# Encoder layer with neighbourhood attention and Fourier mixing: a third Y buffer, an earlier store, earlier squares and a moved scale

## The chip, the cores and the metric

The kernel runs on one core of a Trainium2 chip. The metric is the device time of one execution in microseconds (us); the time of a kernel is the median over its runs. All arithmetic is float32: a matrix product is done as three TensorE products of a high and a low part (high by high, high by low, low by high), so every operand is first split in two by ScalarE (a cast to the rounded type) and VectorE or GpSimd (the remainder). In the profile PE is TensorE, PEld its weight load, DVE is VectorE, ACT is ScalarE, POOL is GpSimd and SP is SyncE, whose queue issues nearly all DMAs.

## The reference

One encoder layer is applied to a prompt of 256 rows and a sample of 2048 rows, each row of width 1024.

```python
def encoder_layer(x, w_in, rpb, w_fourier, b_fourier, g_pre, g_na, g_f, w_out, g_post):
    h = rms_norm(x, g_pre)
    proj = h @ w_in
    q, k, v, z_a, u_f, z_f = jnp.split(
        proj, [NA_WIDTH, 2 * NA_WIDTH, 3 * NA_WIDTH, 4 * NA_WIDTH, 4 * NA_WIDTH + F_WIDTH], axis=-1)
    y_a = neighbourhood_attention(q, k, v, rpb)
    y_f = fourier_mix(u_f, w_fourier, b_fourier)
    mixed = jnp.concatenate([rms_norm(y_a, g_na) * jax.nn.silu(z_a),
                             rms_norm(y_f, g_f) * jax.nn.silu(z_f)], axis=-1)
    out = mixed @ w_out
    return x + rms_norm(out, g_post)
```

`neighbourhood_attention` works on a grid of 64 columns: each position attends to a window of up to 8 rows by 16 columns, with a bias from `rpb` and logits scaled by 1/8. `fourier_mix` takes the real part of a two-dimensional FFT over the sequence and over groups of 64 channels, then multiplies by `w_fourier` and adds `b_fourier`. All four widths (NA_WIDTH, F_WIDTH, and the heads and groups that make them up) come to 512.

## The kernel before, in words

The program is one straight line of instructions. Its stages, with the time at which they run in the profiled execution:

1. **Projections (0 to 555).** The columns of `w_in` are multiplied with the normalised rows. For the prompt this is a loop of 16 steps (the `for b in range(16)` loop at line 749): step `b` makes one block of 128 output columns, and `b // 4` tells which tensor it belongs to (two gates, then k, then q). The weights of step `b` are split two steps ahead by `b_raw(b)` (lines 574 to 584) into `wh` (ScalarE) and `wl` (VectorE; GpSimd for the steps listed in `WP`). For b of 12 and more, the q columns, the split also multiplies by -0.125. The result leaves PSUM through a ScalarE activation (line 783).
2. **Fourier stage two (555 to 580)**, which leaves its spectra in SBUF.
3. **The Y stage (580 to 616).** A loop over four blocks `e` of 128 channels (line 1315). For each block three products `ti` in the order 2, 0, 1 are made by `y_mm` into PSUM (`py`), biased by ScalarE into `t1`, and combined by VectorE into the tile `Y` of 128 x 2304 float32, 1152 KB in all (`comb`, line 1276). The first 256 columns, the prompt's, are stored to DRAM (`yD`) inside `y_out` as soon as `ti` 2 is done (line 1302), the other 2048 after the three (line 1325). `Y` has two buffers, so block 2 overwrites the tile of block 0 and block 3 that of block 1. For the first two blocks and part of the third, the squares of Y are summed into `sqs` (ScalarE squares, GpSimd adds). During block 2 a small tile `y0` is loaded: rows 0 to 127 of the first three Y blocks from `yD` (line 1321) and their gates from `zD` (line 1322). GpSimd multiplies the two (line 1324). During block 3 VectorE adds the fourth block (line 1348), ScalarE and VectorE split `y0` into `y0h` (lines 1350 and 1352), and the scores of the first two attention groups are worked in between. From here on the order on every engine is the order in which the code is written (`manual_schedule`); ahead of it the scheduler of the framework orders ACT, DVE, POOL and SP, while the order on TensorE is always as written.
4. **Attention with the output product of the Fourier half woven in (616 to 850).** `G` is a list of 36 groups (4 pairs of heads by 9: the prompt and 8 pieces of the sample). Step `k` (line 1575) does the transposes of group `k - 2` (`transp`: TensorE into `ptb`, then copies by ScalarE and VectorE into `pt`), the scores and exponentials of group `k`, and the product with v (`pv`). On even steps one output tile of 128 rows (`ftiles`) is multiplied by half of `w_out`: `f_mm` into two PSUM tiles, `f_evac` into `ofs`, stored to `oD`. The inputs of a tile are loaded by `ys_load` (`yr` from `yD`, `yz` from `zD`), multiplied by GpSimd (`ys_mul`) and split (`y_hi` on ScalarE, `y_lo` on VectorE). `pv` leaves a closure in `pending`, which `run_squares` calls in the next step: it squares the `pv` result on ScalarE. The PSUM slot of `pv` (tag "c") is a single one, so the next `pv` waits for that square.
5. **The attention half of the output product and the residual (850 to 947).**

The weights that stage 4 reads first, `wo1`, are loaded in two halves of 2 MB (`load_wo1(0)`, `load_wo1(1)`, line 1227), together with the bias table `tb` of the first pair of heads (`load_t(0, 1)`) and the q tiles of groups 2 and 3 (`prep`). All of them are issued on SP ahead of the Y stage.

Of the kernel before, what the change touches and what calls it, by code (L numbers as in the profile page):

```python
# [10 lines left out]
F32 = mybir.dt.float32  # L11
F32R = mybir.dt.float32r
AF = mybir.ActivationFunctionType
ALU = mybir.AluOpType
# [3 lines left out]
TP, TS = 256, 2048  # L18
T = TP + TS
# [6 lines left out]
NG = 13  # L26
NK = 16
BP = (3, 5)
WP = (7, 9, 11)

HALF = ((0, 28), (4, 8), (12, 16), (20, 24))
KW = (24, 32, 32, 24)
# [143 lines left out]
def build(tc, A, O):  # L176
    nc = tc.nc
# [396 lines left out]
    def b_raw(b):  # L574
        wh, wl = [gt(BS, F32R, "w" + x) for x in "hl"]
        src = wp_[b]
        if b < 12:
            nc.scalar.copy(wh, src)
            (nc.gpsimd if b in WP else nc.vector).tensor_tensor(out=wl, in0=src, in1=wh.bitcast(F32), op=ALU.subtract)
        else:  # L580
            nc.scalar.activation(wh, src, AF.Copy, scale=-0.125)
            nc.vector.scalar_tensor_tensor(out=wl, in0=src, scalar=-0.125, in1=wh.bitcast(F32), op0=ALU.mult,
                                           op1=ALU.subtract)
        wb[b] = wh, wl


# [162 lines left out]
    for b in range(16):  # L749
        kind, blk = divmod(b, 4)  # L750
        if b < 10:
            wz_load(1)
        if b in (0, 2):
            n_load((b // 2, 1))
        if b == 10:
            op_load(0)
        if b == 12:
            op_load(1)
        if b < 14:
            b_raw(b + 2)  # L760
        if b < 8:
            x, y = divmod(b, 2)
            n_scale(None, *divmod(x, 2)[::-1], range(2 * y, 2 * y + 2))
        elif b < 12:
            n_sum(b - 8)
        if b in (3, 5, 12, 13):
            n_first((3, 5, 12, 13).index(b))
        if b > 13:
            op_split(b - 14)
        p = mmt(512)[:, :TP]  # L770
        wh, wl = wb.pop(b)
        for k in range(KC):
            mm3(nc, p, wh[:, k], wl[:, k], hp_[:, k], lp_[:, k], k == 0, k == KC - 1)
        o = st.tile([128, 256], F32, tag="f", name="f", bufs=3)
        if kind == 1:
            v = [(o, p)]
        elif kind == 3:
            v = [(o[:, 128 * x:128 * x + 128].rearrange("p (x r c) -> p r x c", x=2, c=16),
                  p[:, 128 * x:128 * x + 128].rearrange("p (r x c) -> p r x c", x=2, c=16)) for x in range(2)]
        else:  # L780
            v = [(o.rearrange("p (r b c) -> p b r c", b=2, c=32), p.rearrange("p (b r c) -> p b r c", b=2, c=32))]
        for d, i in v:
            nc.scalar.activation(d, i, AF.Silu if kind < 2 else AF.Copy)
        if kind < 2:
            nc.sync.dma_start(zD[kind, blk * 128:blk * 128 + 128, :TP], o)
        else:
            nc.sync.dma_start((kD if kind == 2 else qD)[blk, :, :TP], o)
# [297 lines left out]
    def load_t(pr, kind):  # L1085
        t = TB[pr, kind] = tp.tile([128, 2400], F32, tag="tb", name="tb", bufs=2)
        if kind == 0:
            nc.sync.dma_start(t[:, :512], A["tp"][pr])
            nc.sync.dma_start(t[:, 512:1792].rearrange("p (h x) -> p h x", h=2), tD[pr][:, :, :640])
        else:  # L1090
            nc.sync.dma_start(t[:, :1760].rearrange("p (h x) -> p h x", h=2), tD[pr][:, :, 640:])
# [18 lines left out]
    def prep(g):  # L1110
        pr = g["pr"]
        ql = g["q"] = jl.tile([128, 256], F32, tag="q", name="q", bufs=4)
        if g["R"] is None:
            nc.sync.dma_start(ql, qD[pr, :, :TP])
            return
        for x, n, r in halves(g):
            t0 = TP + 1024 * (r // 16) + 512 * g["hc"]
            q = qD[pr, :, t0:t0 + 512].rearrange("p (b x) -> p b x", b=2)[:, :, 16 * (r % 16):16 * (r % 16) + n // 2]
            nc.sync.dma_start(ql.rearrange("p (b x) -> p b x", b=2)[:, :, x // 2:x // 2 + n // 2], q)
# [107 lines left out]
    def load_wo1(n):  # L1227
        for c in range(4):
            wo1[n].append(gt([128, 2, 512], F32R, "wo1"))
            nc.sync.dma_start(wo1[n][c].bitcast(F32),  # L1230
                              woD[1, :, c, :, n * 512:n * 512 + 512].rearrange("x p d -> p x d"))

    load_wo1(0)
    for g in G[:2]:
        prep_v(g)
    load_wo1(1)
    load_t(0, 1)
    prep(G[2])
    prep(G[3])
    pg = ExitStack()  # L1240
    sm = pg.enter_context(tc.tile_pool(name="smY", bufs=2))
    sqy = pq_.enter_context(tc.tile_pool(name="sqy", bufs=1, side="right"))
# [70 lines left out]

    order = ExitStack()
    for e in range(4):
        Y = sqy.tile([128, T], F32, tag="Y", name="Y", bufs=2)
        if e < 3:
            for ti in (2, 0, 1):
                y_out(e, ti, *y_mm(e, ti))
                if e == 2 and ti == 2:  # L1320
                    nc.sync.dma_start(y0[:, 0, :3], yD[1, :3, :, :128].rearrange("c p t -> p c t"))
                    nc.sync.dma_start(y0[:, 1], zD[0, :, :128].rearrange("(c p) t -> p c t", p=128))
                if e == 2 and ti == 0:
                    nc.gpsimd.tensor_tensor(out=y0[:, 0, :3], in0=y0[:, 0, :3], in1=y0[:, 1, :3], op=ALU.mult)
            nc.sync.dma_start(yD[1, e, :, TP:], Y[:, TP:])
            if e == 2:
                Y2 = Y
            for i in range(T // SQ if e < 2 else 1):
                ts = slice(i * SQ, i * SQ + SQ)
                if e == 0:  # L1330
                    nc.scalar.activation(sqs[:, ts], Y[:, ts], AF.Square)
                elif e == 2:
                    sq = sm.tile([128, SQ], F32, tag="sqf", name="sqf", bufs=2)
                    nc.scalar.activation(sq[:, :TP], Y[:, :TP], AF.Square)
                    nc.gpsimd.tensor_tensor(out=sqs[:, :TP], in0=sqs[:, :TP], in1=sq[:, :TP], op=ALU.add)
                else:
                    sq = sm.tile([128, SQ], F32, tag="sqf", name="sqf", bufs=2)
                    nc.scalar.activation(sq, Y[:, ts], AF.Square)
                    nc.gpsimd.tensor_tensor(out=sqs[:, ts], in0=sqs[:, ts], in1=sq, op=ALU.add)
            continue  # L1340
        order.enter_context(tc.manual_schedule(engines=MAN))
        py = y_mm(e, 2)
        scores(G[0])
        first_soft(G[0], lambda: y_out(e, 2, *py))
        py = y_mm(e, 0)
        y0h = gt([128, 2, 4, 128], F32R, "y0h")
        y0h = [y0h[:, 0], y0h[:, 1]]
        nc.vector.tensor_tensor(out=y0[:, 0, 3], in0=Y[:, :128], in1=y0[:, 1, 3], op=ALU.mult)
        sq = sm.tile([128, SQ], F32, tag="sqf", name="sqf", bufs=2)
        y_out(e, 0, *py, lambda: (nc.scalar.copy(y0h[0], y0[:, 0]),  # L1350
                                  nc.scalar.activation(sq[:, :TP], Y[:, :TP], AF.Square)))
        nc.vector.tensor_tensor(out=y0h[1], in0=y0[:, 0], in1=y0h[0].bitcast(F32), op=ALU.subtract)
        soft(G[0], 0)
        soft(G[0], 1)

        nc.sync.dma_start(y0[:, 0], yD[1, :, :, 128:256].rearrange("c p t -> p c t"))
        nc.sync.dma_start(y0[:, 1], zD[0, :, 128:256].rearrange("(c p) t -> p c t", p=128))
        scores(G[1])
        py = y_mm(e, 1)
        first_soft(G[1])  # L1360
        nc.vector.tensor_tensor(out=sqs[:, :TP], in0=sqs[:, :TP], in1=sq[:, :TP], op=ALU.add)
        soft(G[1], 0)
        y_out(e, 1, *py)
# [60 lines left out]
    def ys_split(d):  # L1424
        y_hi(d)
        y_lo(d)
# [25 lines left out]
    def f_evac(d, n):  # L1452
        t, p = d["t"], d.pop(("p", n))
        if n == 0:
            d["o"] = gt([128, D], F32, "ofs")
        o = d["o"]
        ns = slice(n * 512, n * 512 + 512)
        if n:
            nc.scalar.activation(o[:, ns], p, AF.Copy, scale=invf[:, t:t + 1])
            nc.sync.dma_start(oD[t * 128:t * 128 + 128, :], o)  # L1460
        else:
            V.tensor_scalar(o[:, ns], p, invf[:, t:t + 1], None, ALU.mult)
# [34 lines left out]
    def run_squares():  # L1497
        while pending:
            pending.pop()()
# [56 lines left out]
    ftiles[0]["h"], ftiles[0]["l"] = y0h  # L1556
    y_parts(ftiles[1])
    ftiles[1]["raw"], ftiles[1]["z"] = y0[:, 0], y0[:, 1]
    nc.sync.dma_start(yD[1, 3, :, TP:], Y[:, TP:])
    f_mm(ftiles[0], 0)  # L1560
    f_norm(range(2))
    ys_mul(ftiles[1])
# [4 lines left out]
    f_evac(ftiles[0], 0)  # L1567
    f_mm(ftiles[0], 1)
    ys_split(ftiles[1])
    f_evac(ftiles[0], 1)  # L1570
    ys_load(ftiles[2])
    prep_v(G[2])
    prep(G[4])
    prep(G[5])
    for k in range(2, len(G) + 2):
# [14 lines left out]
        if 24 <= k < 32:  # L1590
            y = k - 24
            nc.sync.dma_start(WO[y % 2][:, y // 2].bitcast(F32), woD[0, y % 2, y // 2])
        x = k // 2
        transp(f)
        run_squares()
        if k % 2:
# [189 lines left out]
```

## Time and profile before

| what | value |
|---|---|
| time, median of 3 runs | 941.89 us (940.89 to 943.53) |
| the profiled execution's own time | 949.42 us |
| its span, first to last instruction | 947.64 us |
| mean granted TensorE clock over the span | 0.992 |
| TensorE busy | 930.8 us of the span |
| VectorE, ScalarE, GpSimd busy | 667.6, 470.1, 342.2 us |
| moved by DMA | 265.0 MB, mean 280 GB/s |

The page gives busy times by engine, the chain of work that ended last, and the costliest groups. A line such as `603.37 0.66 PE L171 MATMUL py<-abh,pqh ... [3.78 <-DVE Y L1276]` in the timeline is read so: it starts 603.37 us after the span's start, lasts 0.66 us, writes `py` from `abh` and `pqh`, and its engine was idle for 3.78 us before it until an instruction of VectorE that writes `Y` at line 1276 released it. Columns of a window table are the stretch, its length, busy time of each engine with the number of instructions, the granted TensorE clock (1.00 is full speed), the busy share of the DMA engines and what they moved per second.

### The profile page before, as it was taken

The page shows a single profiled execution, that of the slowest core. Times are in us where ns is not written, and L with a number is a line of the kernel's source. Part 1 is how long each engine was busy: PE and PEld are TensorE (multiplying, and loading weights), DVE is VectorE, ACT ScalarE, POOL GpSimd, SP SyncE. Part 2 cuts the span into 40 slices and gives each one's busy share as a digit, 9 for nine tenths or more (in the row PEclk, how much of TensorE's full clock was granted, in tenths as well). Part 3 has the DMA queues.
Part 4 walks back from the last instruction along what each step waited for, and adds up shares of the span by engine and source line. Part 5 has one row for each costly group of instructions (what it writes and reads, how often), then busy time and mean ns, then how long its engine had stood idle before and what let it go on. Part 6 is the DMA issues. An engine that isn't in the chain of part 4 may idle for free. (4 is left out here: it accounts for less than half of the span.)

```text
span 947.6 us, 18877 instructions
## 1 busy us (share of the span) xinstructions
PE 930.8 (98%) x6774; PEld 778.4 (82%) x6774; DVE 667.6 (70%) x1305; ACT 470.1 (50%) x1038; POOL 342.2 (36%) x339
## 2 busy tenths in 40 slices
PE   9999999999999999999999999899999999999996
PEld 7889988888888878888888898778788787888885
DVE  5478998688865967697666545468566665659997
ACT  5846677532323643233344235467566666654443
POOL 2201302435650300453343100345456665424444
PEclk9999999999999999999999999899999999999999
DMA  8899777468664999759979788678788899879993
GB/s 317 329 358 375 236 249 283 161 231 313 227 261 182 359 394 332 275 199 316 316 278 323 256 318 272 244 241 271 246 246 271 263 292 283 266 228 371 338 344 124
DMA packets 146717, 265.02 MB, mean 280 GB/s; under 512 B 21880, under 2 KB 86648, under 8 KB 143744
## 3 DMA queue, kind: packets, MB, share of 16 engines
q1 hardware_dynamic: 146464, 263.79, 80.2%
q8 instruction: 54, 0.88, 0.4%
q14 instruction: 39, 0.32, 0.1%
q10 hardware_dynamic: 160, 0.02, 0.0%
HBM read 175.21 MB, written 95.88 MB: 286 GB/s over the span
## 5 line engine op out<-in xcount | busy, mean ns | idle before, releaser
L171 PE MATMUL mm<-xh,wa 128*128 128x512 f32 x448 | 174.4, 389 | 0.0
L173 PE MATMUL mm<-xh,wa 128*128 128x512 f32 x448 | 174.3, 389 | 0.0
L172 PE MATMUL mm<-xl,wa 128*128 128x512 f32 x448 | 174.3, 389 | 0.0
L171 PEld LDWEIGHTS mm<-xh,wa 128*128 128x128 f32 x448 | 84.1, 188 | 17.5
L173 PEld LDWEIGHTS mm<-xh,wa 128*128 128x128 f32 x448 | 84.1, 188 | 17.5
L172 PEld LDWEIGHTS mm<-xl,wa 128*128 128x128 f32 x448 | 84.1, 188 | 17.2
L548 POOL TENSOR_TENSOR ws<-wr 128x512 f32<-128x512 f32 x16 | 22.4, 1402 | 183.5 <-DMA wr<-wz 115.0
L1431 PE MATMUL ptb<-wo,yh 128*128 128x512 f32 x272 | 86.8, 400 | 0.0
L1431 PE MATMUL po<-w,yh 128*128 128x512 f32 x280 | 86.6, 391 | 0.0
L1215 POOL TENSOR_SCALAR w<-w,m 128x352 f32<-128x352 f32 (+4 forms) x136 | 74.9, 570 | 28.8 <-PE s L1181 14.2
L563 DVE TENSOR_TENSOR wa<-wr,wa 128x512 fp32r<-128x512 f32 x60 | 57.1, 959 | 30.7 <-ACT wa L562 30.7
L1208 ACT ACTIVATE w<-w,m 128x352 f32<-128x352 f32 (+4 forms) x136 | 69.9, 522 | 12.7 <-DVE m L1203 12.4
L867 DVE TENSOR_TENSOR f<-u,mm 128x512 f32<-128x512 f32 x64 | 43.6, 681 | 34.3 <-PE mm L173 29.7
L172 PE MATMUL mm<-vl,xh 128*128 128x512 f32 x168 | 65.6, 390 | 1.0 <-DVE vl L494 1.0
L171 PE MATMUL mm<-vh,xh 128*128 128x512 f32 x168 | 65.4, 389 | 0.0
L173 PE MATMUL mm<-vh,xl 128*128 128x512 f32 x168 | 65.4, 389 | 0.0
L1431 PEld LDWEIGHTS ptb<-wo,yh 128*128 128x128 f32 x272 | 49.3, 188 | 14.8 <-ACT sqa L1538 3.4
L1431 PEld LDWEIGHTS po<-w,yh 128*128 128x128 f32 x280 | 52.2, 188 | 10.9
L562 ACT CAST wa<-wr 128x512 fp32r<-128x512 f32 x60 | 36.4, 617 | 42.1 <-PE mm L173 21.2
L1510 PEld LDWEIGHTS pv<-pt,v 96*64 96x64 f32 (+2 forms) x1280 | 45.2, 137 | 12.3 <-issue 6.6
L1431 PE MATMUL po<-w,yl 128*128 128x512 f32 x140 | 54.5, 389 | 0.0
L1431 PE MATMUL ptb<-wo,yl 128*128 128x512 f32 x136 | 53.1, 391 | 0.0
(254 smaller groups left out, 2209.5 us busy)
## 6 DMA issues: line engine op xcount, KB each, us to landing
wr<-wz SPq DMA_DIRECT2D x48, 512.0 KB
vl<-sD SPq DMA_DIRECT2D x20, 512.0 KB
xm<-xm SPq DMA_DIRECT2D x9, 1024.0 KB
oD<-ofs SPq DMA_DIRECT2D x18, 512.0 KB
of<-oD SPq DMA_DIRECT2D x18, 512.0 KB
yr<-yD SPq DMA_DIRECT2D x34, 256.0 KB
zD<-f SPq DMA_DIRECT2D x16, 512.0 KB
woD<-wo SPq DMA_DIRECT2D x16, 512.0 KB
```

What stands on the lines that cost most here:

```text
L171: nc.tensor.matmul(out, lh, rh, start=first, stop=False)
L172: nc.tensor.matmul(out, lh, rl, start=False, stop=False)
L173: nc.tensor.matmul(out, ll, rh, start=False, stop=last)
L548: T2 = lambda o, i, j, op: nc.gpsimd.tensor_tensor(out=o, in0=i, in1=j, op=op)
L562: nc.scalar.copy(o[:, 0], src)
L563: nc.vector.tensor_tensor(out=o[:, 1], in0=src, in1=o[:, 0].bitcast(F32), op=ALU.subtract)
L867: nc.vector.tensor_tensor(out=dst(f, b), in0=src(uu[u]), in1=src(p), op=op)
L1208: nc.scalar.activation(w, w, AF.Exp, bias=m[:, h:h + 1], scale=-1.0, accum_out=m[:, 2 + h:3 + h])
L1215: nc.gpsimd.tensor_scalar(w, w, m[:, 4 + h:5 + h], 1.0, ALU.mult, ALU.mult)
L1431: nc.tensor.matmul(p, (d["l"] if x == 2 else d["h"])[:, c], w(n, int(x == 1), c), start=j == 0, stop=j == 11)
L1510: nc.tensor.matmul(p[hs, b, o], v[:nk, b, x, hs], g["pt"][b][:nk, h, j * 128 + o.start:j * 128 + o.stop], start=first, stop=last)
```

## The change

Four edits:

- **Y.** The tile `Y` gets a third buffer. The second half of `wo1`, the table `tb` and the q tiles of groups 2 and 3 are requested after the two stores of Y block 0 instead of ahead of the Y stage. The long store of block 3 is cut into 512 and 1536 columns, and the load of the inputs of tile 2 is issued ahead of the store of tile 0's output.
- **Squares.** In odd steps of stage 4 that lie at the first or second group of a pair of heads (k of 9, 19 and 27), the square of the last `pv` result is placed ahead of the copies of the transposes.
- **q scale.** The weights of the prompt's q are split without a scale, like the others; the factor -0.125 is given to the activation that leaves PSUM.
- **Share of GpSimd.** `WP` gets a fourth entry, so that the remainder of step 13 is made by GpSimd.

```diff
-WP = (7, 9, 11)
+WP = (7, 9, 11, 13)
...
-        if b < 12:
-            nc.scalar.copy(wh, src)
-            (nc.gpsimd if b in WP else nc.vector).tensor_tensor(out=wl, in0=src, in1=wh.bitcast(F32), op=ALU.subtract)
-        else:
-            nc.scalar.activation(wh, src, AF.Copy, scale=-0.125)
-            nc.vector.scalar_tensor_tensor(out=wl, in0=src, scalar=-0.125, in1=wh.bitcast(F32), op0=ALU.mult,
-                                           op1=ALU.subtract)
+        nc.scalar.copy(wh, src)
+        (nc.gpsimd if b in WP else nc.vector).tensor_tensor(out=wl, in0=src, in1=wh.bitcast(F32), op=ALU.subtract)
...
-            nc.scalar.activation(d, i, AF.Silu if kind < 2 else AF.Copy)
+            nc.scalar.activation(d, i, AF.Silu if kind < 2 else AF.Copy, scale=-0.125 if kind == 3 else 1.0)
...
-    load_wo1(1)
-    load_t(0, 1)
-    prep(G[2])
-    prep(G[3])
...
-        Y = sqy.tile([128, T], F32, tag="Y", name="Y", bufs=2)
+        Y = sqy.tile([128, T], F32, tag="Y", name="Y", bufs=3)
...
             nc.sync.dma_start(yD[1, e, :, TP:], Y[:, TP:])
+            if e == 0:
+                load_wo1(1)
+                load_t(0, 1)
+                prep(G[2])
+                prep(G[3])
...
-    nc.sync.dma_start(yD[1, 3, :, TP:], Y[:, TP:])
+    for x in (slice(TP, TP + 512), slice(TP + 512, T)):
+        nc.sync.dma_start(yD[1, 3, :, x], Y[:, x])
...
     ys_split(ftiles[1])
+    ys_load(ftiles[2])
     f_evac(ftiles[0], 1)
-    ys_load(ftiles[2])
...
+        if k % 2 and g and i < 2:
+            run_squares()
         transp(f)
         run_squares()
```

Two places show how the order moves. The first is the queue of SP in the Y stage; `yD<-Y 128x256` is a store of a block's prompt columns, `yD<-Y 128x2048` that of the rest, `wo_...<-woD` the second half of `wo1`, `y_...` the small tile `y0`. Before:

```order
L1091 DMA tb<-tD 128x2x880
L1119 DMA q<-qD 128x2x64 x2
L1119 DMA q<-qD 128x2x128
L1302 DMA yD<-Y 128x256
L1325 DMA yD<-Y 128x2048
L1302 DMA yD<-Y 128x256
L1325 DMA yD<-Y 128x2048
L1302 DMA yD<-Y 128x256
L1322 DMA y_5180<-zD 128x4x128
L1321 DMA y_5180<-yD 128x3x128
L1325 DMA yD<-Y 128x2048
```

In the changed kernel the same part of SP's queue reads (the four `wo` loads stand between the first two stores and the table):

```order
L1293 DMA yD<-Y 128x256
L1316 DMA yD<-Y 128x2048
L1225 DMA wo_5240<-woD 128x2x512
L1225 DMA wo_5242<-woD 128x2x512
L1225 DMA wo_5244<-woD 128x2x512
L1225 DMA wo_5246<-woD 128x2x512
L1086 DMA tb<-tD 128x2x880
```

and, after the q loads and the stores of block 1, around the loads of `y0`:

```order
L1293 DMA yD<-Y 128x256
L1313 DMA y_5165<-zD 128x4x128
L1316 DMA yD<-Y 128x2048
L1312 DMA y_5165<-yD 128x3x128
L1293 DMA yD<-Y 128x256
```

The stores of block 0 now stand ahead of the second half of `wo1`, and the load of `y0` from `yD` stands behind the long store of block 2, where it stood ahead of it.

The second place is VectorE in steps 10 to 15 of the prompt's projections; `wl` is the remainder of a step's weights, `nx` and `nt` are sums for the sample's projections that follow. Before:

```order
L439 TENSOR_TENSOR nx<-nx 128x2048
L582 SCALAR_TENSOR_TENSOR wl<-wr,wh 128x1024
L439 TENSOR_TENSOR nx<-nt,nx 128x2048
L582 SCALAR_TENSOR_TENSOR wl<-wr,wh 128x1024
L439 TENSOR_TENSOR nx<-nx 128x2048
L582 SCALAR_TENSOR_TENSOR wl<-wr,wh 128x1024
```

In the changed kernel:

```order
L439 TENSOR_TENSOR nx<-nx 128x2048
L578 TENSOR_TENSOR wl<-wr,wh 128x1024
L439 TENSOR_TENSOR nx<-nt,nx 128x2048
L439 TENSOR_TENSOR nx<-nx 128x2048
L578 TENSOR_TENSOR wl<-wr,wh 128x1024
```

The second of these remainders has left VectorE; GpSimd has a fourth one in its place.

## The prediction

> **What bounds the kernel now.** TensorE is busy for 930.8 of 947.64 us (the table above), so I read the view of who waited for whom on TensorE first, and then the timeline around the longest wait.
>
> ```profile
> PE py L171 <- DVE Y L1276: 3.8, 1, 3.8
> PE ptb L1488 <- ACT ofs L1459: 1.1, 1, 1.1
> PE mm L173 <- DVE wl L582: 0.4, 2, 0.2
> PE pv L1510 <- ACT ysq L1534: 0.2, 1, 0.2
> PE pv L1510 <- ACT sqa L1538: 0.2, 1, 0.2
> ```
>
> Only what shortens TensorE's idle time, or raises its clock, can shorten the run by much. The waits are few (the columns are total, times, longest, in us), and each part of the change touches one of these rows. The timeline of the longest, SP's rows first:
>
> ```profile
> 584.14 2.56 SPq L1230 DMA_DIRECT2D wo<-woD  x4
> 593.23 0.72 SPq L1325 DMA_DIRECT2D yD<-Y  x1
> 601.89 2.34 DVE L1276 TENSOR_TENSOR Y<-t,py 128x252 f32<-128x252 f32 x10 [6.72 <-DMA yD<-Y]
> 599.25 0.34 PE L1263 MATMUL py<-a,w 96*128 96x384 f32 x1
> 603.37 0.66 PE L171 MATMUL py<-abh,pqh 128*128 128x384 f32 x1 [3.78 <-DVE Y L1276]
> 615.69 2.92 PE L1431 MATMUL ptb<-wo,y0h 128*128 128x512 f32 x12
> ```
>
> Block 2 must write the buffer of block 0, whose store was issued at 593.23, behind four `wo` loads, and landed only near 601.9. VectorE waits, the `py` banks stay full, and TensorE idles for 3.78. The stretches of 4 us show what else it costs:
>
> ```profile
> 584.00:588.00 4.00, 4.00 (x25) 4.00 (x24) 2.39 (x8) 1.23 (x3) 0.00 (x0) 1.00 1.02 268
> 588.00:592.00 4.00, 4.00 (x24) 4.00 (x24) 1.98 (x13) 3.38 (x9) 0.00 (x0) 1.00 0.94 251
> 596.00:600.00 4.00, 3.59 (x21) 3.26 (x19) 0.00 (x0) 2.50 (x8) 3.90 (x6) 1.00 1.04 413
> 600.00:604.00 4.00, 0.63 (x2) 0.66 (x3) 2.11 (x9) 1.32 (x3) 1.65 (x3) 0.72 0.49 200
> 604.00:608.00 4.00, 4.00 (x14) 4.00 (x13) 1.50 (x8) 0.08 (x1) 0.81 (x2) 0.50 0.59 178
> 608.00:612.00 4.00, 4.00 (x34) 3.58 (x34) 2.13 (x16) 2.30 (x10) 0.75 (x1) 0.92 0.56 231
> ```
>
> The last three columns are the granted clock, the busy share of the DMA engines and GB/s. The clock falls to half during the idle stretch and stays there until past 608. What is lost is 4 x 0.28 + 4 x 0.50 + 4 x 0.08 = 3.44 us. So the wait costs 3.78 + 3.44 = **7.22 us**. The same rows show the other fact that counts: from 584 to 600 the DMA engines are fully busy.
>
> **Third buffer and early store.** With three buffers block 2 writes a free tile, so the 7.22 go. Block 3 takes over the tile of block 0, whose store is now ahead of the `wo` loads and long landed. Without the wait TensorE would reach the first output product (615.69 above) at 615.69 - 7.22 = 608.5. What is late next is `y0`, which that product reads:
>
> ```profile
> 587.03 1.28 DVE L1276 TENSOR_TENSOR Y<-t,py 128x378 f32<-128x378 f32 x6 [1.19 <-PE py L173]
> 607.74 1.01 POOL L1324 TENSOR_TENSOR y<-y 128x384 f32<-128x384 f32 x1 [3.19 <-DMA y<-yD]
> 612.35 0.62 ACT L1350 CAST y0h<-y 128x512 fp32r<-128x512 f32 x1
> 613.54 0.69 DVE L1352 TENSOR_TENSOR y0h<-y,y0h 128x512 fp32r<-128x512 f32 x1
> 614.54 0.35 DVE L1203 CUSTOM_DVE_ANT_1 sc<-ptb,tb 128x192 f32<-128x192 f32 x1
> ```
>
> From the landing of the last part of `y0` it takes the multiply (1.01), the cast (0.62), and then VectorE from the remainder to the end of the bias step that frees the PSUM tile (613.54 to 614.89, 1.35): 3.0 us. For TensorE not to wait, `y0` must have landed by 608.5 - 3.0 = 605.5. Before, it had over 3 us to spare, because the stall had let the queue run empty (0.49 busy above). Now it has not. SP issues in order; block 0 is complete at 588.3, so the `wo` loads start some 4 us later than at 584.14, and until the `y0` data comes the queue has to carry:
>
> ```profile
> yD<-Y SPq DMA_DIRECT2D x3, 1024.0 KB
> wo<-woD SPq DMA_DIRECT2D x4, 512.0 KB
> tb<-tD SPq DMA_DIRECT2D x1, 880.0 KB
> yD<-Y SPq DMA_DIRECT2D x3, 128.0 KB
> y<-zD SPq DMA_DIRECT2D x1, 256.0 KB
> y<-yD SPq DMA_DIRECT2D x1, 192.0 KB
> q<-qD SPq DMA_DIRECT2D x2, 64.0 KB
> q<-qD SPq DMA_DIRECT2D x1, 128.0 KB
> ```
>
> That is all of it but the first 128 KB store: 3072 + 2048 + 880 + 256 + 256 + 192 + 256 = 6960 KB, 7.13 MB, from about 589.0. The long store of block 2 is in it, because the new order puts the `y0` load behind that store. At the 413 GB/s of the row 596 to 600 it takes 17.3 us (606.3); at 260, the mean of the two rows in which the `wo` loads ran, 27.4 us (616.4). I take each kind at its own row: `wo`, 2.10 MB at 260, 8.1 us, and 5.03 MB at 413, 12.2 us. `y0` lands at 609.3, **3.8 us** too late (ends: 0.8 and 10.9). SP, VectorE and ScalarE stand in order behind it: the cast blocks the exponentials of the second group and, through the remainder, its bias steps, so the wait appears in front of the first output product. A wait as long as the old one I charge with the old clock loss, 3.44 (ends: 0 and 3.44). The sum of this part is -7.22 + 3.8 + 3.44 = **0.0 us**.
>
> On the clock, the trace has it falling when TensorE had been idle for 2.2 us (599.59 to 601.8, from the 0.72 above). [...]
>
> **Split store and earlier load of tile 2.**
>
> ```profile
> 628.57 1.28 POOL L1408 TENSOR_TENSOR yr<-yr,yz 128x512 f32<-128x512 f32 x1 [3.44 <-DMA yz<-zD]
> 630.41 0.68 ACT L1459 ACTIVATE ofs<-ptb,invf 128x512 f32<-128x512 f32 x1
> 631.15 0.46 PE L1488 MATMUL ptb<-ident,sc 64*128 64x64 f32 x7 [1.05 <-ACT ofs L1459]
> ```
>
> TensorE waits 1.05 because ScalarE empties the output tile late, which had stood behind the cast of tile 2, whose gates (`yz`) landed at 628.6. The short store lets SP pass to that load sooner, and the order no longer puts it behind the store of tile 0. I take the whole **1.05** (ends: 0 and 1.05). The extra DMA costs SP one issue, 0.72 at most by the row at 593.23, with nothing urgent behind it.
>
> **q scale and GpSimd.** The stretches of 20 us around the prompt's q:
>
> ```profile
> 100.00:120.00 20.00, 19.43 (x159) 18.83 (x157) 19.96 (x13) 13.23 (x20) 4.07 (x2) 1.00 0.64 200
> 120.00:140.00 20.00, 19.79 (x98) 16.55 (x97) 17.76 (x15) 13.78 (x17) 0.00 (x0) 1.00 0.73 251
> 102.57 3.74 POOL L579 TENSOR_TENSOR wl<-wr,wh 128x1024 fp32r<-128x1024 f32 x1 [2.23 <-ACT wh L578]
> 107.21 1.05 ACT L581 ACTIVATE wh<-wr 128x1024 fp32r<-128x1024 f32 x1
> 111.72 1.21 DVE L582 SCALAR_TENSOR_TENSOR wl<-wr,wh 128x1024 fp32r<-128x1024 f32 x1
> ```
>
> VectorE is full (19.96 of 20) and TensorE idles 0.57 + 0.21 = 0.78 us behind it. One remainder of 1.21 goes to GpSimd, and VectorE is that much earlier for the rest, which covers four waits of about 0.2. I take the whole **0.78** (ends: 0 and 0.78). On GpSimd it takes 3.74; it needs `wh` of step 13, the row at 107.21, so it starts near 108.3 and ends near 112.0, while VectorE had it ready at 112.9, when TensorE had just begun to wait. That cover is 0.9; if it goes, each us beyond it is paid. The scale itself is free: the activation it moves to exists already, and multiplication by a power of two leaves the split as it was.
>
> **Squares.** In the three short steps:
>
> ```profile
> 670.02 0.85 ACT L1491 COPY pt<-ptb 96x384 f32<-96x384 f32 x2 [1.30 <-PE ptb L1488]
> 671.22 1.59 PE L1510 MATMUL pv<-pt,v 96*64 96x128 f32 x40 [0.21 <-ACT ysq L1534]
> ```
>
> The square (0.39) stood behind two copies of 0.43 each, and `pv` waited for it. Moved ahead it runs in the 1.30 in which ScalarE was idle, as far as VectorE is done with `pv`, and the copies end up to 0.39 later, at 671.3. The first half of the 40 products (0.8 us) needs the first copy alone, so the second is covered. I take the two recorded waits, **0.4** (ends: -0.4, if the copies become what `pv` waits for, and 0.8).
>
> **The sum**, against the profiled execution's own 949.42 us: 0.0 - 1.05 - 0.78 - 0.4 = -2.2, so 947.2. The median of the runs shown is 941.89, 7.5 below that execution; its span alone (947.64) is longer than the slowest run (943.53). I carry the difference over: 941.89 - 2.2 = **939.7**.
>
> **The rivals.**
>
> *The load keeps up.* If the queue runs at 413 GB/s throughout, `y0` is 0.8 late and no clock is lost: -7.22 + 0.8 - 2.23 = -8.65, 933.2; if it is in time, 932.4. For it: 413 held for 4 us with `wo`, `tb` and stores mixed, and the `wo` loads would now stand behind a long store instead of starting alone. Against it: 268 and 251 while the engines were busy all the same. Chance 0.17.
>
> *A short new wait that leaves the clock alone.* A wait of about 2.5 us at the first output product, idle in parts too short for the throttle: -7.22 + 2.5 - 2.23 = -6.95, 934.9. For it: the 1.05 at 631.15 left the clock at full speed. Against it: the fall after 2.2 us above. [...] Chance 0.13.
>
> *The wait of block 2 is not in the timed runs.* The gap of 7.5 between that execution and the median is nearly the 7.22 of this one wait; an execution without the profiler's own traffic may land the store sooner and not wait. Then only the small terms are left, 941.89 - 2.23 = 939.7, and the change does not do what its first part says. Against it: nothing in one profile can tell this from a general slowdown. Chance 0.18.
>
> *Slower: the `y0` load behind the long store.* One place, the queue between 589 and the landing of `y0`. If it moves 7.13 MB at 260 GB/s, `y0` lands at 616.4, TensorE waits 10.9 and loses the clock: -7.22 + 10.9 + 3.44 - 2.23 = +4.9, 946.8. Break-even is a wait of 6.0 (321 GB/s); it is slower by over 0.3% from a wait of 8.9, a landing at 614.4, under 281 GB/s. For it: the `wo` rows. Against it: stores ran at 413. Chance 0.15.
>
> **How the numbers follow.** My forecast, a wait handed from `Y` to `y0` at about the same price, has chance 0.37, from 936.5 to 942.5 as the new wait and its clock loss vary. 0.3% of 941.89 is 2.8 us, about what a measurement of this kernel can tell from no change. Faster by more than that: 0.09 of the forecast, 0.13, 0.17 and 0.02 of the third rival, 0.41 in all. Slower by more: 0.13 of the last and 0.02 of the forecast, 0.15. The rest, 0.44, is within. The range, 932.0 to 944.0, leaves out about half of the last rival and the lower edge of the first. The time is that of the forecast, 939.7.
>
> **What would show it.** In the new profile, VectorE's first write of Y block 2 must follow its `py` without the 6.7 us behind `yD<-Y`. If I am right, the longest wait on TensorE stands instead before `ptb<-wo,y0h`, 3 to 5 us long, with GpSimd's `y<-y` multiply behind `DMA y<-yD` near 609, and a stretch of half clock there. If the multiply starts by 605.5, the first rival holds and the gain is near 9. The waits of `mm` on `wl`, of `ptb` on `ofs` and of `pv` on `ysq` and `sqa` should be gone; a wait of `mm` on POOL would show that the cover of 0.9 was too thin. A profiled span near 945.5 with a median near 942 would show that the timed runs never had what the profile shows.

## The result, and the profile after

| | before | changed |
|---|---|---|
| median, same chip | 942.94 us (11 runs, 940.89 to 946.88) | 946.34 us (11 runs, 945.26 to 949.89) |
| span of the profiled execution | 947.64 us | 944.5 us |
| its own time | 949.42 us | 946.34 us |
| its mean granted clock | 0.992 | 0.994 |

The ratio of the runs is 1.0039 (95% interval 1.0024 to 1.0053): the change makes the kernel **slower by 0.39%**, 3.4 us between the medians, outside the range predicted (932.0 to 944.0). Yet the two profiled executions say the opposite: the changed one is 3.1 us shorter. The kernel before was profiled in an execution 6.5 us above its own median, the changed one in an execution at its median. Two of all timed executions stand apart, one of the kernel before (2364 us) and one of the run `y3early` (5245 us); the ratios leave them out.

TensorE's waits in the changed kernel (total, times, longest, in us; the three rows that bear on the change), and the wait of SP's queue ahead of the `y0` load:

```profile
PE ptb L1427 <- issue: 4.3, 1, 4.3
PE mm L173 <- DVE wl L578: 1.0, 2, 0.8
...
PE ptb L1176 <- ACT pt L1487: 0.2, 1, 0.2
```

```profile
SPq L1312 <- DMA yD<-Y: 3.4, 1, 3.4
```

The wait for `Y` is gone and a longer one stands before the first output product. The timeline around it, the queue of SP first, then GpSimd, ScalarE, VectorE and TensorE:

```profile
583.31 0.32 SPq L1293 DMA_DIRECT2D yD<-Y  x1
586.52 0.32 SPq L1316 DMA_DIRECT2D yD<-Y  x1
586.88 3.32 SPq L1225 DMA_DIRECT2D wo<-woD  x4
595.94 0.32 SPq L1293 DMA_DIRECT2D yD<-Y  x1
601.18 0.32 SPq L1316 DMA_DIRECT2D yD<-Y  x1
605.02 0.37 SPq L1312 DMA_DIRECT2D y<-yD  x1
608.76 0.99 POOL L1315 TENSOR_TENSOR y<-y 128x384 f32<-128x384 f32 x1 [8.38 <-DMA y<-yD]
609.78 0.62 ACT L1346 CAST y0h<-y 128x512 fp32r<-128x512 f32 x1 [5.67 <-POOL y L1315]
610.43 0.69 DVE L1348 TENSOR_TENSOR y0h<-y,y0h 128x512 fp32r<-128x512 f32 x1 [3.39 <-ACT y0h L1346]
611.90 5.04 PE L1427 MATMUL ptb<-wo,y0h 128*128 128x512 f32 x12 [4.29 <-issue]
```

This is the chain that the prediction described: the `y0` load comes late, GpSimd's multiply starts at 608.76 (the load was forecast to land at 609.3), and multiply, cast, remainder and bias step take 3.1 us more until TensorE goes on. The wait reads "issue": the view names no releaser for it. The stretches of 4 us (clock, DMA share and GB/s in the last three columns) show what else there is:

```profile
584.00:588.00 4.00, 4.00 (x25) 4.00 (x24) 1.79 (x9) 2.15 (x6) 0.00 (x0) 1.00 0.30 112
592.00:596.00 4.00, 4.00 (x24) 4.00 (x23) 2.62 (x13) 1.80 (x5) 1.72 (x3) 1.00 1.05 399
608.00:612.00 4.00, 0.10 (x1) 0.12 (x1) 1.56 (x8) 1.38 (x4) 1.61 (x3) 0.69 0.01 3
612.00:616.00 4.00, 4.00 (x10) 3.13 (x11) 2.19 (x12) 2.00 (x9) 2.73 (x6) 0.50 0.44 131
```

From 584 to 588 the DMA engines were busy for 0.30 of the time: SP stood until 586.52, when block 0 was complete, and the `wo` requests were queued behind that store. Once the store was through, the `wo` loads ran at 399 GB/s, not at the 260 assumed. The `y0` load was issued only at 605.02: SP held it for 3.4 us, until block 2's short store, issued at 595.94, had landed. At half clock the twelve products took 5.04 us; the same group took 2.92 in the prediction's rows, so half clock cost 2.1 us here, on top of the 4.3.

Two questions were open: why the timed runs lose what the profiles seem to gain, and what makes `y0` late.

### The profile page after: what moved, and what is told of

Same layout as the page of the kernel before. It is cut to its first block, busy times and chain, and to the rows that moved or that the text cites. A ratio compares the mean times of both kernels' runs of the same rounds, so it can differ in the third digit from the quotient of the medians.

```text
span 944.5 us, 18878 instructions
## 1 busy us (share of the span) xinstructions
PE 928.8 (98%) x6774; PEld 776.2 (82%) x6774; DVE 671.3 (71%) x1304; ACT 469.7 (50%) x1038; POOL 341.9 (36%) x340
## 4 chain that ended last, share of the span: by engine, by line
PE 93%; DMA 3%; DVE 2%; issue 1%; ACT 1%; POOL 0%; DVEq 0%; SPq 0%; ACTq 0%
PE mm L173 18%; PE mm L172 18%; PE mm L171 18%; PE ptb L1427 11%; PE po L1427 10%; PE pv L1506 5%; PE ptb L1484 3%; PE s L1176 2%; PE pab L1006 2%; PE ptb L1176 2%; DMA yD<-Y 1%; DMA wo<-woD 1%; DVE nx L439 0%; DMA rv<-wv 0%; PE ppq L1045 0%
```

## The experiments

### The kernel before once more, the Y part alone, the rest alone, and the change without its q part

`ctl` is the kernel before, unchanged. `y3early` is the kernel before with three Y buffers and the early store alone:

```diff
-    load_wo1(1)
-    load_t(0, 1)
-    prep(G[2])
-    prep(G[3])
...
-        Y = sqy.tile([128, T], F32, tag="Y", name="Y", bufs=2)
+        Y = sqy.tile([128, T], F32, tag="Y", name="Y", bufs=3)
...
+            if e == 0:
+                load_wo1(1)
+                load_t(0, 1)
+                prep(G[2])
+                prep(G[3])
```

`rest` is the kernel before with every other line of the change's diff (squares, q scale, `WP`, split store). `noq` is the changed kernel with the q part undone:

```diff
-WP = (7, 9, 11, 13)
+WP = (7, 9, 11)
...
+        if b < 12:
+            nc.scalar.copy(wh, src)
+            (nc.gpsimd if b in WP else nc.vector).tensor_tensor(out=wl, in0=src, in1=wh.bitcast(F32), op=ALU.subtract)
+        else:
+            nc.scalar.activation(wh, src, AF.Copy, scale=-0.125)
+            nc.vector.scalar_tensor_tensor(out=wl, in0=src, scalar=-0.125, in1=wh.bitcast(F32), op0=ALU.mult,
+                                           op1=ALU.subtract)
...
-            nc.scalar.activation(d, i, AF.Silu if kind < 2 else AF.Copy, scale=-0.125 if kind == 3 else 1.0)
+            nc.scalar.activation(d, i, AF.Silu if kind < 2 else AF.Copy)
```

Expected of `ctl`:

> The kernel before, unchanged, for further times and a further profile of it. Theory A (the timed runs of before rarely hold block 2's wait for its Y buffer; the 7.2 us of it in the first profile came with slow wo loads, 2.1 MB in 8 us): median 942 to 944; in the new profile the wait of the product that wants Y is 0 to 2 us and the span 939 to 943. Theory B (the wait of 3.8 us is in every run of before and the change loses its time elsewhere): the wait stands in the new profile as well at 3 to 4 us with half clock behind it, and the span is near 947.

Expected of `y3early`:

> The kernel before with only three Y buffers and the early long store (load of wo, tb and q moved behind it); squares, q scale and the split store as before. Theory A: the old wait was mostly absent from the timed runs, the new one for the y0 load (4.3 us and 2 to 3.4 us of half clock) is in each: 3 to 6 us slower than before, so 946 to 949, and slower than the whole change by the 1 us of the split store. Theory B (the Y part is even, the loss is in the q scale and the squares): within 1 us of before. The longest wait in the new profile is that of the first product with wo and y0h, 4 to 5 us.

Expected of `rest`:

> The kernel before with the other three parts alone: q scaled at evacuation with GpSimd's fourth remainder, squares ahead of copies in three steps, the split store; two Y buffers and the old place of the loads. Theory A: -1.0 (split store) +0.3 (q) -0.1 (squares): 0 to 1.5 us faster than before. Theory B: 2 to 4 us slower than before.

Expected of `noq`:

> The change with the q scale and GpSimd's fourth remainder undone. My theory for the q part, from the two profiles: step 14's wait for VectorE's remainder (0.84 us) goes, and the difference to the whole change is 0.2 to 1.0 us faster. By the prediction's own term it would be 0.8 us slower than the whole change.

Measured, each against the kernel before on the same chip (median 944.70, 35 runs):

| run | median us | ratio (95%) | profiled execution, us | longest wait of TensorE in the Y stage |
|---|---|---|---|---|
| ctl | 942.12 | 0.9987 (0.9967 to 1.0007) | 941.43 | 1.58, on Y |
| y3early | 947.69 | 1.0035 (1.0020 to 1.0050) | 947.22 | 4.1, on y0 |
| rest | 942.47 | 0.9982 (0.9960 to 1.0004) | 943.64 | 1.87, on Y |
| noq | 946.15 | 1.0015 (1.0002 to 1.0029) | 946.03 | 4.3, on y0 |

The new profile of the kernel before, now at 941.43 us, the fastest of its 12 runs and 0.7 below their median; timeline of SP, GpSimd and TensorE, then the stretches:

```profile
581.48 1.92 SPq L1230 DMA_DIRECT2D wo<-woD  x4
587.28 1.17 SPq L1325 DMA_DIRECT2D yD<-Y  x1
601.39 0.37 SPq L1321 DMA_DIRECT2D y<-yD  x1
604.09 1.09 POOL L1324 TENSOR_TENSOR y<-y 128x384 f32<-128x384 f32 x1 [5.11 <-DMA y<-yD]
597.79 0.41 PE L171 MATMUL py<-abh,pqh 128*128 128x384 f32 x1 [1.58 <-DVE Y L1276]
607.73 2.92 PE L1431 MATMUL ptb<-wo,y0h 128*128 128x512 f32 x12
623.19 0.46 PE L1488 MATMUL ptb<-ident,sc 64*128 64x64 f32 x7 [1.06 <-ACT ofs L1459]
```

```profile
584.00:588.00 4.00, 4.00 (x25) 4.00 (x24) 2.28 (x13) 3.12 (x9) 0.00 (x0) 1.00 0.94 312
588.00:592.00 4.00, 4.00 (x24) 4.00 (x23) 2.37 (x9) 1.55 (x4) 0.81 (x1) 1.00 1.05 395
596.00:600.00 4.00, 2.42 (x15) 2.24 (x14) 3.14 (x12) 1.67 (x5) 2.83 (x4) 1.00 0.75 281
600.00:604.00 4.00, 4.00 (x36) 3.57 (x35) 2.55 (x20) 2.32 (x10) 0.00 (x0) 1.00 0.49 166
```

The old wait is 1.58 us here, not 3.78, and the clock does not fall. In the first profile the rows between 584 and 592, in which the `wo` loads ran, show 268 and 251 GB/s, here 312 and 395, and the store of block 0 was issued at 587.28 instead of 593.23. Some 3.4 of these 6.0 us are a lead of the whole program, for block 0 was complete at 584.9 here and at 588.3 there; the other 2.6 are the transfers ahead of the store, and the wait is 2.2 shorter. Of the 12 timed runs of `ctl`, 9 lie between 941.4 and 943.7 at a granted clock of 0.997 or 0.998, 3 between 946.9 and 948.4 at 0.993 to 0.995. That those 3 held the long wait with its half clock, as the first profile (0.992) did, fits, but was not seen: only one execution of a set is profiled. The mean clock points the same way, though it counts a half clock wherever in the run it lies: it is 0.996 or less in 43 of the 105 further runs of the kernel before, `ctl` included, and in all 11 runs of the changed kernel.

Two sets of the same kernel can differ as well: `ctl` has a median of 942.12, the 35 other runs of the kernel before in that session 944.70, spread without a gap from 941.7 to 948.2. So `rest` and `noq` tell little by their times. `y3early` is clear of that: all its runs but the 5245 lie between 946.8 and 948.6. It alone is slower by 0.35%, about the whole loss; `rest` is not slower. So the loss is in the Y part, and what the change removes in an execution like those of `ctl` and `rest` is a wait of 1.6 to 1.9 us, not 7.2.

### What makes y0 late: a third buffer alone, the y0 load ahead, the wo requests ahead

`y3`, against the kernel before:

```diff
-        Y = sqy.tile([128, T], F32, tag="Y", name="Y", bufs=2)
+        Y = sqy.tile([128, T], F32, tag="Y", name="Y", bufs=3)
```

`first`, against the changed kernel; the requests now open the hand-ordered part, and GpSimd's product of `y0` moves into it with its place on GpSimd unchanged:

```diff
-                if e == 2 and ti == 2:
-                    nc.sync.dma_start(y0[:, 0, :3], yD[1, :3, :, :128].rearrange("c p t -> p c t"))
-                    nc.sync.dma_start(y0[:, 1], zD[0, :, :128].rearrange("(c p) t -> p c t", p=128))
...
-            nc.sync.dma_start(yD[1, e, :, TP:], Y[:, TP:])
+            if e < 2:
+                nc.sync.dma_start(yD[1, e, :, TP:], Y[:, TP:])
...
+        nc.sync.dma_start(y0[:, 1], zD[0, :, :128].rearrange("(c p) t -> p c t", p=128))
+        nc.sync.dma_start(y0[:, 0, :3], yD[1, :3, :, :128].rearrange("c p t -> p c t"))
+        nc.sync.dma_start(yD[1, 2, :, TP:], Y2[:, TP:])
```

`mid`, against the changed kernel:

```diff
+    load_wo1(1)
     pg = ExitStack()
...
             if e == 0:
-                load_wo1(1)
```

Expected of `y3`:

> The kernel before with a third Y buffer alone: the requests for wo, tb and q stay ahead of block 0's long store, as before. Theory C (the y0 load is late because those requests stand behind the long store of block 0 in SyncE's queue, so that the transfers lie idle at 584 to 588 us and wo, tb and q come behind it): without that idle stretch y0 is late only by its place behind block 2's long store, 0.5 to 2.5 us and little or no half clock; median 940 to 944, 4 to 7 less than y3early. Rival (any third buffer makes it late, since block 2's long store goes ahead of the y0 load): the wait is again near 4 us, 946 to 948.

Expected of `first`:

> The whole change, with the y0 load ahead of block 2's long store in SyncE's queue, nothing else moved. Theory C: the load still has to wait for block 2's short store, which lands behind wo, tb and q; it is issued near 604.5 to 605 as before and lands only some 1 us sooner: wait 3 to 3.6 us instead of 4.3, time 0.7 to 2 us below the whole change (944 to 945.6). Rival (the long store is what makes it late): wait under 1 us, no half clock, 939 to 942.

Expected of `mid`:

> The whole change with only the four wo requests put back to their old place ahead of block 0's long store; tb and q stay behind it. Theory C (the transfers lie idle at 584 to 588 us, share 0.30, since SyncE waits for block 0 with the wo requests queued behind): the idle stretch is filled, y0 comes 2 to 3 us sooner, the wait is 1 to 2.5 us with at most 1.5 us of half clock; median 942 to 944.5, 2 to 4 us below the whole change. Rival (the order of the requests does not matter, only the bytes ahead of y0): wait near 4 us, 946.

| run | median us | ratio to before (95%) | block 2's short store / y0 load issued at | wait on y0, us | the 12 products, us |
|---|---|---|---|---|---|
| changed kernel | 946.34 | 1.0039 (1.0024 to 1.0053) | 595.94 / 605.02 | 4.29 | 5.04 |
| first | 946.45 | 1.0022 (1.0010 to 1.0033) | 596.62 / 605.47 | 3.34 | 5.46 |
| mid | 944.85 | 1.0001 (0.9984 to 1.0019) | 596.56 / 603.85 | 2.32 | 4.59 |
| y3 | 943.34 | 0.9988 (0.9976 to 1.0001) | 594.27 / 600.21 | 1.79 | 4.58 |

The first output product in `first`, `mid` and `y3`, from their timelines:

```profile
611.54 5.46 PE L1427 MATMUL ptb<-wo,y0h 128*128 128x512 f32 x12 [3.34 <-issue]
```

```profile
610.76 4.59 PE L1427 MATMUL ptb<-wo,y0h 128*128 128x512 f32 x12 [2.32 <-issue]
```

```profile
600.21 0.37 SPq L1321 DMA_DIRECT2D y<-yD  x1
607.94 4.58 PE L1431 MATMUL ptb<-wo,y0h 128*128 128x512 f32 x12 [1.79 <-issue]
```

In `first` SP issues the `y0` load ahead of block 2's long store, but no sooner than before, at 605.47: it reads what block 2's short store writes, and that store (596.62) lands behind `wo`, `tb`, q and the stores of block 1; SP waits 7.1 us for it. The place behind the long store costs only the 1 us by which the wait gets shorter. The half clock took back 0.4 us of that in the profile, and the median did not follow (946.45, where 944.0 to 945.6 was expected); a rest of 0.5 us is too small to be seen between sets that were not timed together. Putting the requests back, first `wo`, then all of them, shortens the wait to 2.32 and 1.79. `mid` came out 0.35 above what was expected; in its profile half clock cost 1.7 us, where at most 1.5 was expected. So **the early store is what costs**: it holds SP until block 0 is complete, and 3184 KB of requests pass through the queue later, ahead of the short store that the `y0` load depends on. The third buffer alone (`y3`) trades 1.6 us on `Y` for 1.8 on `y0` and 1.7 of half clock; in the times it cannot be told from the kernel before.

### Both causes taken away, with and without the q part

`fix` has three buffers with the requests at their old place, the `y0` load ahead of block 2's long store as in `first`, the split store and the squares of the change, and the q part of before. `fixq` has the q part of the change as well. `fixwp3` is `fixq` with GpSimd's fourth remainder taken back. `fix_b` and `fixq_b` are `fix` and `fixq` again. `fix` against `first`, beside the q part of before that `noq` shows:

```diff
+    load_wo1(1)
+    load_t(0, 1)
+    prep(G[2])
+    prep(G[3])
     pg = ExitStack()
...
-            if e == 0:
-                load_wo1(1)
-                load_t(0, 1)
-                prep(G[2])
-                prep(G[3])
```

`fixwp3`, against `fixq`:

```diff
-WP = (7, 9, 11, 13)
+WP = (7, 9, 11)
```

Expected of `fix`:

> Three Y buffers with the old place of the requests for wo, tb and q, the y0 load ahead of block 2's long store, the split store and the squares of the change, the q part of before. If both causes are taken away no wait over 0.5 us is left between 595 and 615: 942 (the kernel before without half clock) -1.6 (its short wait for Y) -1.3 (split store) -0.1 (squares) = 939, between 938 and 940.5, with less spread than before. If the wait for Y or y0 comes back in another place: 941 to 944.

Expected of `fixq`:

> The same with the q part of the change (scale at evacuation, GpSimd's fourth remainder). By the profiles (GpSimd's remainder beside VectorE's product, step 14 waits): 0.7 to 1.2 us slower than the one with the q part of before. By the prediction's term: 0.8 us faster.

Expected of `fixwp3`:

> The faster kernel (old place of the requests, y0 load ahead) with q scaled at evacuation, but GpSimd's fourth remainder back on VectorE. If GpSimd's remainder beside VectorE's product is what costs in the q part: VectorE's product of 128x2048 at 107 us takes 2.3 us instead of 4.5, step 14 does not wait (1.3 us in fixq's profile), and the median is within 0.5 us of fix and 0.5 to 1.3 us below fixq_b. If the scale at evacuation itself costs: as slow as fixq_b.

Expected of `fix_b`:

> The faster kernel again, with the q part of before: 939 to 941, no wait over 0.5 us at 595 to 615 us, 2.5 to 4 us below the kernel before.

Expected of `fixq_b`:

> The same with the whole q part of the change, again: 0.5 to 1.3 us slower than fix_b, with step 14 waiting 0.8 to 1.3 us. By the prediction's term 0.8 us faster than fix_b.

| run | median us | range | ratio to before (95%) | wait of step 14, us |
|---|---|---|---|---|
| fix (6 runs) | 939.96 | 939.12 to 941.88 | 0.9953 (0.9937 to 0.9969) | none |
| fixq (7 runs) | 940.92 | 939.27 to 942.23 | 0.9957 (0.9941 to 0.9973) | 1.28 |
| fixwp3 (12) | 940.56 | 938.31 to 942.81 | 0.9966 (0.9949 to 0.9982) | none |
| fix_b (12) | 940.41 | 938.39 to 941.83 | 0.9960 (0.9945 to 0.9976) | none |
| fixq_b (12) | 941.23 | 939.28 to 943.03 | 0.9972 (0.9955 to 0.9988) | 1.14 |

The first two were timed against 943.87 for the kernel before, the other three against 943.51. The timeline of `fix` at the Y stage:

```profile
601.31 0.37 SPq L1339 DMA_DIRECT2D y<-yD  x1
604.00 1.01 POOL L1345 TENSOR_TENSOR y<-y 128x384 f32<-128x384 f32 x1 [4.17 <-DMA y<-yD]
607.16 2.98 PE L1431 MATMUL ptb<-wo,y0h 128*128 128x512 f32 x12
```

No wait and no half clock here (0.58 us of wait in `fix_b`'s profile, 1.1 in `fixq`'s), and a version **0.4 to 0.5% faster than the kernel before**, which is faster than both; all 18 of its runs lie between 938.4 and 941.9, so the executions of 946 and more are gone too.

For the q part, VectorE's row at 108 us in `fixwp3`, then VectorE, GpSimd and TensorE in the changed kernel, then two of VectorE's sums in the first profile of the kernel before:

```profile
108.19 2.28 DVE L439 TENSOR_TENSOR nx<-nt,nx 128x2048 f32<-128x2048 f32 x1
```

```profile
107.61 4.49 DVE L439 TENSOR_TENSOR nx<-nt,nx 128x2048 f32<-128x2048 f32 x1
107.38 2.57 POOL L578 TENSOR_TENSOR wl<-wr,wh 128x1024 fp32r<-128x1024 f32 x1 [2.98 <-ACT wh L577]
115.61 0.39 PE L173 MATMUL mm<-ph,wl 128*128 128x256 f32 x1 [0.84 <-DVE wl L578]
```

```profile
101.75 2.28 DVE L439 TENSOR_TENSOR nt<-nx 128x2048 f32<-128x2048 f32 x1
104.07 4.39 DVE L439 TENSOR_TENSOR nx<-nx 128x2048 f32<-128x2048 f32 x1
```

With GpSimd's remainder beside it, VectorE's sum of 128x2048 takes 4.49 us, without it 2.28. The loss of 2.21 is nearly what was left of GpSimd's instruction when VectorE's began (107.38 + 2.57 - 107.61 = 2.34). GpSimd's remainder at 102.57 in the kernel before, which the prediction read as 3.74 us of work, began while VectorE's sum ran until 104.03, and ended 2.28 us after it (102.57 + 3.74 = 106.31). The remainder that GpSimd takes off VectorE is 1.21 us. In time, the medians of `fix_b` and `fixq_b` differ by 0.8 us in the expected direction, and `fixwp3`, where step 14 does not wait, is 0.15 above `fix_b` and 0.67 below `fixq_b`, as expected of GpSimd's instruction and not of the scale. But the intervals overlap: the profiles show the q part's wait, the times do not resolve it. In `noq` too the wait of step 14 is gone, with 0.2 us between its median and the change's, on sets of runs that were not timed together.

## Why the prediction was wrong

**The step that failed** is "I carry the difference over: 941.89 - 2.2 = 939.7". It took a sum made against one execution and applied it to a median whose runs mostly do not hold the largest term of that sum. In the first profile the wait and its half clock were there; in the profiles of `ctl` and `rest` the term is 1.6 to 1.9, while the new wait, 4.1 to 4.3, is in all three profiles whose Y stage is ordered as in the change (the changed kernel, `y3early`, `noq`). The gap of 7.5 us between the profiled execution and the median was a sign. That it nearly equals the one term is chance: matched instruction by instruction, TensorE in the first profile is 3.3 us behind `ctl` before the Y stage and loses only 4.6 more in it, 2.2 by the wait and 2.4 by half clock.

**The third rival had the condition and the wrong price.** It said that the wait of block 2 is not in the timed runs, and concluded that only the small terms are left. But the new wait does not depend on the old one. With its own numbers it should have read 941.89 + 7.24 - 2.23 = 946.9; the median is 946.34. That this comes so close is partly luck, for it leaves out the 1.6 saved and takes the new wait's clock and the small gains too large. Its sign, "a profiled span near 945.5 with a median near 942", missed by the same step: the span came at 944.5 and the median at 946. Nor is there a sign that profiling itself makes the wait: `ctl`'s profiled execution is the fastest of its set.

**The second rival's term,** a wait of about 2.5 us that costs no clock, is shown by no run: the wait of 2.32 in `mid` and that of 1.79 in `y3` had half clock behind them (4.59 and 4.58 us for the twelve products), and the longest wait in the Y stage that cost no clock is the 1.87 of `rest`.

**The Y part against the profile it was made from** was right in its sum, by two errors that cancel: predicted -7.22 + 7.24 = 0.0; TensorE's start of the first output product moved from 615.69 to 611.90, and the twelve products took 5.04 instead of 2.92, so that it was done 1.7 us sooner; TensorE was 1.8 us ahead already when it came to the Y stage. In its terms:

- *The new wait:* 3.8 predicted, 4.29 measured, through the chain that was named. The path to it was only half right: `wo` ran at 399 GB/s and not at 260, which should have brought the load in sooner, but SP did not issue it before block 2's short store had landed (the 3.4 us above), and the prediction priced the bytes in the queue alone.
- *The clock loss:* 3.44 predicted, 2.1 measured on the products behind the new wait. The working charged half clock also for time in which TensorE was idle anyway, in the old wait (2.4 by the match with `ctl`, so 6.2 in place of 7.22) and in the new one.
- *The y0 load behind the long store* was said to matter; `first` shows about 1 us of wait, and no time.
- *The last rival's break-even,* a wait of 6.0, is 317 GB/s (7.13 MB from 589 to 611.5), not 321; nothing rests on it.

**Split store:** -1.05 predicted, measured -1.06: the wait of 1.06 at 623.19 in `ctl` has no counterpart in the changed kernel, and stands at 1.0 in `y3early`, which lacks the split. It is not gone for good: `fixq`'s profile has the split and a wait of 0.99 at that place, `fixq_b`'s, the same kernel, has none.

**q scale and GpSimd:** -0.78 predicted, the whole idle time of two stretches, of which the view of waits put only 0.4 down to `wl`; step 14 waits 0.84 in the change and 1.1 to 1.3 in `fixq` and `fixq_b`. The step that failed is "VectorE is that much earlier for the rest": VectorE loses 2.2 us in the sum beside GpSimd's remainder (4.49 against 2.28) and saves 1.21. The prediction feared GpSimd for its own lateness (the cover of 0.9) and did not ask what VectorE's sum takes beside GpSimd's remainder, though the profile before held a row of 4.39 us for a sum of the same size beside GpSimd's instruction at 102.57.

**Squares:** -0.4 predicted. The waits of `pv` on `ysq` and `sqa` are gone, and in their place step 9 and step 27 come later by the copies of the transposes (`ptb` on `pt`, 0.2 in the waits), which now stand behind the square on ScalarE. Matched instruction by instruction against `ctl`, TensorE's lag changes by +0.24 and -0.29 at each of the two places: under 0.1 us in all. No run has the squares alone.

From `ctl` to the changed kernel these rows sum to -1.58 (Y) + 4.29 + 2.12 (y0 and clock) + 0.84 (q) - 1.06 (split) = +4.6; the spans of these two executions differ by 4.9, the medians (946.34 and 942.12, not timed together) by 4.2, and those of the runs that were timed together by 3.4.

## What to carry over

Before a term of a profile is subtracted from a median, see whether the profiled execution's own time is near that median; where there is a gap, price the change once with the longest wait and once without it, and leave every new wait in both. A store that was moved ahead in SP's queue held back the requests behind it until its data was complete (586.52 here, with the DMA engines busy for 0.30 of 584 to 588); count the idle stretch of the transfers, and follow what must be read back from DRAM. Before an instruction goes to GpSimd, see in the profile what VectorE's instructions take beside one like it: the sum here took 4.49 us instead of 2.28.

## What the runs showed of the hardware

- VectorE's sum of 128x2048 took 2.28 or 2.29 us in the rows at 101 to 115 us where GpSimd had no remainder under way when it began, and 4.38 to 4.50 where it had, before and after the change.
- In the Y stage half clock lasted 3.41 us in `y3` and `noq` (the rows below) and 3.4 in `mid`, and 6.83 in the first profile of the kernel before (601.79 to 608.62) and in the changed kernel (609.48 to 616.31), 6.8 in `y3early` and in `first`; the 3.4 and 6.8 are worked out from the clock of stretches of 4 us. The rows of `y3`, `noq` and `rest` (TensorE's busy time follows the length, the clock is the third column from the end):

```profile
605.29:608.70 3.41, 1.62 (x8) 1.20 (x7) 2.23 (x12) 2.04 (x7) 1.77 (x5) 1.00 0.06 16
608.70:612.11 3.41, 3.41 (x9) 2.67 (x8) 1.52 (x8) 1.33 (x5) 2.24 (x4) 0.50 0.46 138
```

```profile
605.57:608.99 3.42, 1.80 (x11) 1.47 (x9) 1.21 (x4) 0.00 (x0) 0.50 (x1) 1.00 0.41 134
608.99:612.40 3.41, 0.77 (x3) 0.67 (x4) 2.24 (x12) 2.05 (x7) 1.78 (x5) 1.00 0.06 16
612.40:615.81 3.41, 3.41 (x10) 2.63 (x9) 1.51 (x8) 1.32 (x5) 2.14 (x4) 0.50 0.46 138
```

```profile
597.29:600.71 3.42, 2.15 (x13) 1.82 (x11) 0.89 (x6) 2.56 (x6) 3.42 (x6) 1.00 1.01 419
600.71:604.12 3.41, 2.81 (x16) 2.84 (x17) 2.52 (x11) 0.72 (x3) 1.34 (x2) 1.00 0.65 214
```

- The length of a wait did not tell what clock it cost. The 1.79 us of `y3` brought twelve products from 2.92 to 4.58 us, the 1.87 of `rest` cost no clock, and half clock lasted 3.41 us in `noq`, with a wait of 4.3, as in `y3`. Nor did TensorE's busy time in the stretch ahead: in `noq` full clock followed a stretch with 1.80 us busy, while at the start of the first profile half clock (7.87 to 11.28) followed one with 2.06 (4.46 to 7.87). What makes the clock fall is not shown.
- The transfers of one kernel take a different time in different executions: the store of block 0, which stands behind the four `wo` loads, was issued 4.9 us after its data was complete in the first profile of the kernel before and 2.4 us after in `ctl`; the old wait was 3.78 us in the one and 1.58 in the other.
